# A decoder trunk on one core: output weights gated and summed in the stream's background track, and the output gate's row built by VectorE plus two rounded column sums

## The chip, the core and the metric

The kernel runs on one NeuronCore of one Trainium2 chip. A core has a matrix engine (TensorE, "PE" in the profile; its weight loads stand apart as "PEld"), a vector engine (VectorE, "DVE"), a scalar engine (ScalarE, "ACT"), GpSimd ("POOL") and a sync engine ("SP") that here only issues DMA transfers. POOL issues DMA transfers as well. Each engine works through its own list of instructions in order; semaphores tie the lists together. The metric is the device time of one launch in microseconds, as the median of several runs.

## The reference

One layer on a sequence of 1024 positions with 1024 channels, all in float32, cut to what matters here:

```python
mod = c_act @ ada_w[l] + ada_b[l]                    # c_act = silu(c)
shift, scale, gate = jnp.split(mod, 3, axis=-1)
h = rms_norm(x, norm_w[l]) * (1.0 + scale[:, None, :]) + shift[:, None, :]
proj = h @ w_in[l]                                   # 1024 x 9232
hq, hf, hi, hz, gq, gk, gv, gz, ga, mg = jnp.split(proj, IN_OFFSETS, axis=-1)
y_h = hgrn2_branch(hq, hf, hi, hz, ...)              # 8 heads, gated linear recurrence
y_g = gla_branch(gq, gk, gv, gz, ga, ...)            # 4 heads, gated linear attention
u_h = y_h @ w_branch[l, 0]
u_g = y_g @ w_branch[l, 1]
mg = jax.nn.sigmoid(mg.reshape(B, T, N_BRANCH, D_MODEL))
merged = mg[:, :, 0] * u_h + mg[:, :, 1] * u_g
x = x + gate[:, None, :] * (merged @ w_out[l])
return rms_norm(x, final_norm_w)
```

The change touches the vector `gate`, one row of 1024 numbers, and `w_out`, a 1024 x 1024 matrix. Since `gate` scales the columns of `merged @ w_out`, the kernel multiplies it into the columns of `w_out`.

## The kernel before

Activations lie transposed, 128 channels by 1024 positions. A float32 matrix product is made of three products in a rounded type (`fp32r`): `split()` (L190) rounds a tile on ScalarE (L196, the `hi` part) and takes the rest on VectorE (L197, the `lo` part), and then hi*hi, hi*lo and lo*hi are summed in PSUM.

The program has three parts. First comes a start written in a fixed order, in which `h` and the first products are made. Then comes the **stream** (`Stream.go`): a list of jobs, each a block of the product `h @ w_in`. A `Feat` job (L541) makes 128 channels in 48 matrix instructions; a `Vblk2` job (L643 to L645) makes values of four heads in 192. `go` walks through the jobs and, at each unit of work, calls `weave`, which advances two tracks of generators: `stream.side`, in which the attention of the heads is computed, and `stream.back`, the background track. An entry of a track gives back how many units it wants to wait. Only the first entry of a track is advanced; the next begins when it has ended. Tiles come from `S`, 46 slots of 4 KB per partition, handed out in the order in which they were given back; `ahead` loads the weights of coming jobs while enough slots are free.

Before the change the background track holds `prepare()` (sums for a later stage, whose stores to DRAM are the rows `ws`), and behind it `gate_side()`, which makes the gate's row: eight loads of `ada_w`, eight multiply-adds on VectorE (L1052, L1054) into `gacc`, and then, for each half of 512 columns, two plain float32 matrix instructions (L1062: the column sums of `gacc` with a matrix of ones; L1063: the bias row with a row of ones) and a copy to SBUF (L1064).

The last part, `last_stages` and `out_stage`, makes the remaining products by Strassen-like sums of quarters, 28 groups of (b, p). Its matrix instructions stand at L1343 (`b` 0 to 3) and L1520 (the output product). What happens beside them is hung on points of this walk with `after(b, p, i, f)`. There stands, before the change, the work on `w_out`: for each half kk, `load_wy` loads four tiles of 128 x 1024 through SP (L1466), `gate_wy` multiplies each by the gate's row on VectorE (L1474), `sum_wy` makes four sums in place (L1484), and `keep_wy` stores seven of these tiles to DRAM through POOL (L1469, rows `wo`). Half 0 is hung on group (0, 3) and what follows, half 1 on (1, 1) to (1, 7). The output stage reads the seven products of each half back, from group (3, 7) on.

Around them in this part: the sigmoid gates of branch 1 are made on ScalarE from PSUM (L1414) into half slots, and stored by POOL (L1415, rows `gate`); a half slot can be used again when its store has landed. `build` makes the two parts of an activation factor (L1260 to L1264), `prep_duo` those of a weight (L1285, L1286).

An attention (`attention`) of a head needs, on VectorE, the products L676 to L679 before its first block of small matrix instructions (L683), and L710, L711 before the second (L715). `put_act` stores a head's result through POOL (L916, rows `yh`), and POOL adds its squares (L1107).

Past the start, the order of each engine's list is not the order of the code: a scheduler places the instructions by its own estimates. Calls wrapped in `tc.keep_in_program_order` are held to the code's order.

## Time and profile before

| | before |
|---|---|
| median of 3 runs | 1215.93 us (1215.64 to 1216.92) |
| the profiled execution's own time | 1216.46 us |
| its span, first to last instruction | 1214.8 us |
| TensorE granted clock, mean | 0.998 |
| PE busy | 1184.1 us, 97% |
| VectorE, ScalarE, POOL busy | 790.9, 546.9, 123.8 us |
| HBM read and written | 132.87 and 49.28 MB |

The span is the time inside of which the profile has instructions; 1.66 us of the profiled execution lie around it. Times in the rows are microseconds from the start of the span. A matrix instruction's busy time overlaps its neighbours': what it costs on PE is the distance from its start to the start of the next one. "Idle before" is the time for which the instruction's engine had nothing to do, and the arrow names what ended it.

### The profile page before, as it was taken

To read this page: it belongs to the slowest core of one execution; us is meant where nothing else is said; L and a number is where in the kernel's file an instruction comes from. 1 tells how busy PE (TensorE), PEld (TensorE's weight loads), DVE (VectorE), ACT (ScalarE), POOL (GpSimd) and SP (SyncE) were. 2 spreads that over 40 slices of the span, in tenths; PEclk is the share of its full clock that TensorE was granted. 3 is DMA by queue.
4 is the path that set the end of the run, shared out by engine and by line. 5 is a ranking of instruction groups with operands and counts; after the bars stand their busy time and mean duration, and the time that the engine had idled before them with its cause. 6 is when DMAs were issued, how large, how long until landed. Compare 5 with 4: busy or idle time off the path is not lost.

```text
span 1214.8 us, 20860 instructions
## 1 busy us (share of the span) xinstructions
PE 1184.1 (97%) x8579; PEld 982.6 (81%) x8579; DVE 790.9 (65%) x1245; ACT 546.9 (45%) x797; POOL 123.8 (10%) x215
## 2 busy tenths in 40 slices
PE   5999999999999999999999999999999999999997
PEld 3777889889798888888887888877778888878886
DVE  4637444774848456877884365794653775988994
ACT  5646732434434244344332324455743544444554
POOL 4100000202111121121110101011220000000000
PEclk9999999999999999999999999999999999999999
DMA  9814000844444267255341112054697746435523
GB/s 320 277 70 139 18 19 19 293 141 161 156 152 149 66 207 249 94 179 169 108 174 47 59 53 70 36 174 158 227 343 277 260 160 208 135 104 173 174 104 122
DMA packets 130961, 183.51 MB, mean 151 GB/s; under 512 B 7467, under 2 KB 97633, under 8 KB 130866
## 3 DMA queue, kind: packets, MB, share of 16 engines
q1 hardware_dynamic: 117250, 136.87, 35.7%
q0 software_dynamic: 13568, 45.31, 9.6%
q8 instruction: 67, 1.10, 0.4%
q14 instruction: 28, 0.23, 0.1%
q10 hardware_dynamic: 48, 0.01, 0.0%
HBM read 132.87 MB, written 49.28 MB: 150 GB/s over the span
## 4 chain that ended last, share of the span: by engine, by line
PE 61%; issue 23%; DVE 3%; ACT 3%; POOL 2%; DMA 1%; POOLq 0%; ACTq 0%; DVEq 0%
PE pd L541 19%; PE pd L1343 9%; PE sc_ps L1343 5%; PE pm L1343 5%; PE pd L1520 3%; PE pd L643 2%; PE pd L644 2%; PE pd L645 2%; PE sc_ps L1520 2%; PE pm L848 1%; PE pd L352 1%; PE pm L829 1%; PE pm L850 1%; PE pm L1520 1%; PE sc_ps L352 1%
## 5 line engine op out<-in xcount | busy, mean ns | idle before, releaser
L541 PE MATMUL pd<-b,b 128*128 128x512 f32 x1632 | 387.4, 394 | 0.0
L541 PEld LDWEIGHTS pd<-b,b 128*128 128x128 f32 x1632 | 302.4, 188 | 64.8 <-issue 1.4
L1343 PE MATMUL pd<-b,b 128*128 128x512 f32 x720 | 173.7, 392 | 4.3 <-ACT b L1414 2.1
L1343 PEld LDWEIGHTS pd<-b,b 128*128 128x128 f32 x720 | 133.7, 188 | 35.7 <-ACT b L1414 3.2
L197 DVE TENSOR_TENSOR b<-b,b 128x1024 fp32r<-128x1024 f32 (+2 forms) x89 | 98.9, 1122 | 83.1 <-ACT b L196 65.4
L196 ACT CAST b<-b 128x1024 fp32r<-128x1024 f32 (+2 forms) x89 | 82.9, 948 | 92.1 <-DVE b L1199 14.6
L1286 DVE TENSOR_TENSOR b<-b,b 128x1024 fp32r<-128x1024 f32 x56 | 68.3, 1224 | 66.9 <-ACT b L1285 52.3
L1285 ACT CAST b<-b 128x1024 fp32r<-128x1024 f32 x56 | 58.3, 1050 | 73.9 <-PE pd L1343 20.6
L1343 PE MATMUL sc_ps<-b,b 128*128 128x512 f32 x324 | 79.4, 391 | 1.0 <-ACT scT L793 1.0
L600 PE MATMUL pd<-b,b 128*128 128x256 f32 x256 | 74.2, 290 | 0.0
L1264 DVE TENSOR_TENSOR b<-b,b 128x1024 fp32r<-128x1024 f32 x48 | 59.2, 1251 | 20.8 <-ACT b L1263 15.1
L602 PE MATMUL pd<-b,b 128*128 128x256 f32 x256 | 72.5, 283 | 0.0
L601 PE MATMUL pd<-b,b 128*128 128x256 f32 x256 | 72.4, 283 | 0.0
L1343 PEld LDWEIGHTS sc_ps<-b,b 128*128 128x128 f32 x324 | 60.3, 188 | 14.6 <-ACT scT L793 1.4
L1343 PE MATMUL pm<-b,b 128*128 128x512 f32 x300 | 72.1, 389 | 0.0
L1263 ACT CAST b<-b 128x1024 fp32r<-128x1024 f32 x48 | 49.9, 1050 | 41.2 <-PE pd L1343 16.0
L1343 PEld LDWEIGHTS pm<-b,b 128*128 128x128 f32 x300 | 56.3, 188 | 11.7
L352 PE MATMUL pd<-b,b 128*128 128x512 f32 x192 | 53.3, 410 | 2.0 <-ACT b L196 0.9
L1201 POOL DMA_DIRECT2D ws<-b x64 | 34.6, 541 | 192.0 <-DVE b L1195 86.5
L735 ACT COPY xb<-b 128x512 f32<-128x512 f32 x48 | 29.4, 620 | 49.4 <-PE sc_ps L715 26.7
L643 PE MATMUL pd<-b,b 128*128 128x512 f32 x128 | 51.3, 401 | 0.0
L644 PE MATMUL pd<-b,b 128*128 128x512 f32 x128 | 50.0, 390 | 0.0
(285 smaller groups left out, 1964.3 us busy)
## 6 DMA issues: line engine op xcount, KB each, us to landing
b<-in_w_in_dram SPq DMA_DIRECT2D x66, 512.0 KB, 4.2
ws<-b POOLq DMA_DIRECT2D x64, 256.0 KB, 3.3
b<-ws SPq DMA_DIRECT2D x32, 512.0 KB, 4.9
b<-in_x_dram SPq DMA_DIRECT2D x16, 512.0 KB, 5.7
b<-in_ada_w_dram SPq DMA_DIRECT2D x32, 256.0 KB, 6.9
b<-in_w_branch_dram SPq DMA_DIRECT2D x16, 512.0 KB, 4.4
b<-h SPq DMA_DIRECT2D x14, 512.0 KB, 4.3
wo<-b POOLq DMA_DIRECT2D x14, 512.0 KB, 5.7
```

The lines of the kernel that those rows point to most:

```text
L196: nc.scalar.copy(hi, src)
L197: nc.vector.tensor_sub(lo, src, hi.bitcast(F32))
L352: nc.tensor.matmul(accs[f], wg(a, d, f), b[d][:, half * 512:half * 512 + 512], start=(d == 0 and n == 0), stop=(d == KT - 1 and n == 2))
L541: nc.tensor.matmul(ps[0:w, th * 512:(th + 1) * 512], a[:, k, 0:w], b[:, th * 512:(th + 1) * 512], start=(k == 0 and n == 0), stop=(k == KT ...
L600: nc.tensor.matmul(o, lh, hi[:, k % 4, :], start=(k == 0), stop=False)
L601: nc.tensor.matmul(o, lh, lo[:, k % 4, :], start=False, stop=False)
L602: nc.tensor.matmul(o, ll, hi[:, k % 4, :], start=False, stop=(k == KT - 1))
L643: nc.tensor.matmul(o, lh, hi[:, k % 2, :], start=(k == 0), stop=False)
L644: nc.tensor.matmul(o, lh, lo[:, k % 2, :], start=False, stop=False)
L1286: nc.vector.tensor_sub(lo, t, hi.bitcast(F32))
L1343: nc.tensor.matmul(o, a[:, sl], c, start=(p in (1, 5) and kt == 0 and n == 0), stop=(kt == 3 and n == 2), skip_group_check=True)
L1520: nc.tensor.matmul(o, a, b, start=(p in (1, 5) and kt == 0 and n == 0), stop=(kt == 3 and n == 2), skip_group_check=True)
```

## The change

The lines below are of the changed kernel; line numbers shift by 3 from L1057 on, and by up to 48 behind `out_weights`. In the changed code the bias add is L1057, the two matrix instructions are L1065 and L1066, their copy L1067, `load_wy` issues at L1225, `keep_wy` at L1228, `gate_wy` multiplies at L1233, `sum_wy` adds at L1242; L1079, L1096, L1107 and L1201 of before are L1082, L1099, L1110 and L1206.

```diff
@@ gate_side()
-        yield 3
+        nc.vector.tensor_add(gacc[0:1, :], gacc[0:1, :], gbias[0:1, :])
+        hi, lo = split(gacc)
+        S.free(gacc, gbias)
+        yield 4
         gate_b[0] = S.get([D])
         for half in range(2):
             sl = slice(half * 512, half * 512 + 512)
             pg = mtile()
-            nc.tensor.matmul(pg, ones, gacc[:, sl], start=True, stop=False)
-            nc.tensor.matmul(pg, ones[0:1, :], gbias[0:1, sl], start=False, stop=True)
+            nc.tensor.matmul(pg, ones_r, hi[:, sl], start=True, stop=False)
+            nc.tensor.matmul(pg, ones_r, lo[:, sl], start=False, stop=True)
             nc.scalar.copy(gate_b[0][:, sl], pg)
-        S.free(gacc, gbias)
+        S.free(hi, lo)
@@ hgrn_v(h), done(v)
             if h == 0:
                 stream.back.append([gate_side(), 4])
+                stream.back.append([out_weights(), 4])
@@ gate_wy(kk, n), sum_wy(kk, n): the same instructions, without keep_in_program_order
-        tc.keep_in_program_order(nc.vector.tensor_mul(
-            t, t, gate_b[0][:, f * 512:f * 512 + 512].unsqueeze(1).to_broadcast([P, 2, 512])))
+        nc.vector.tensor_mul(t, t, gate_b[0][:, f * 512:f * 512 + 512].unsqueeze(1).to_broadcast([P, 2, 512]))
-        tc.keep_in_program_order(nc.vector.tensor_add(wy[dst], wy[dst], wy[other]))
+        nc.vector.tensor_add(wy[dst], wy[dst], wy[other])
@@ new
+    def out_weights():
+        for kk in range(2):
+            while len(S.free_list) < 12:
+                yield 1
+            load_wy(kk)
+            yield 8
+            for n in range(4):
+                gate_wy(kk, n)
+                yield 2
+            yield 4
+            for n in range(4):
+                sum_wy(kk, n)
+                yield 3
+            S.free(*wy.values())
+            wy.clear()
@@ behind out_run and out_after
-    for kk, (lead, first, then) in enumerate((((0, 3, 0), (0, 6), (0, 7)), ((1, 1, 2), (1, 5), (1, 6)))):
-        after(*lead, lambda kk=kk: load_wy(kk))
-        after(*((1, 1, 0) if kk == 0 else (1, 7, 3)), drop_wy)
-        for n in range(4):
-            after(*first, n, lambda kk=kk, n=n: gate_wy(kk, n))
-            after(*then, n, lambda kk=kk, n=n: sum_wy(kk, n))
```

How the lists of the engines change is shown at three places. In the names, `b_` is a tile of a slot, `pd` and `pm` are PSUM tiles, and the numbers only tell tiles apart.

On PE, in the stream, where the gate's row is summed between two blocks of the values' product (`pd_5955` is the block that ends, the next `pd` the one that begins). Before:

```order
L645 MATMUL pd_5955<-b_5711,b_158 128x512
L1062 MATMUL pm_6017<-b_5918,ones 128x512
L1063 MATMUL pm_6017<-b_5919,ones 128x512
L1062 MATMUL pm_6021<-b_5918,ones 128x512
L1063 MATMUL pm_6021<-b_5919,ones 128x512
L643 MATMUL pd_6026<-b_5699,b_143 128x512
```

In the change:

```order
L645 MATMUL pd_5955<-b_5711,b_158 128x512
L643 MATMUL pd_6022<-b_5699,b_143 128x512
L644 MATMUL pd_6022<-b_5700,b_143 128x512
L645 MATMUL pd_6022<-b_5699,b_151 128x512
L643 MATMUL pd_6022<-b_5699,b_144 128x512
L644 MATMUL pd_6022<-b_5700,b_144 128x512
L645 MATMUL pd_6022<-b_5699,b_152 128x512
L1065 MATMUL pm_6030<-b_5999,ones_r 128x512
L1066 MATMUL pm_6030<-b_6000,ones_r 128x512
L1065 MATMUL pm_6034<-b_5999,ones_r 128x512
L1066 MATMUL pm_6034<-b_6000,ones_r 128x512
L643 MATMUL pd_6022<-b_5703,b_145 128x512
```

The four instructions take `hi` (`b_5999`) and `lo` (`b_6000`) in place of `gacc` and the bias, and stand six instructions later.

On VectorE, at the same place of the program: `b_5918` is `gacc`, the L1054 rows are its last multiply-adds, and L690 on belongs to head 4's attention behind its first small products. Before:

```order
L1054 SCALAR_TENSOR_TENSOR b_5918<-b_5942,cs,b_5918 128x1024
L197 TENSOR_TENSOR b_6331<-b_5855,b_6330 128x1024
L1054 SCALAR_TENSOR_TENSOR b_5918<-b_5951,cs,b_5918 128x1024
L1054 SCALAR_TENSOR_TENSOR b_5918<-b_5962,cs,b_5918 128x1024
L1054 SCALAR_TENSOR_TENSOR b_5918<-b_5971,cs,b_5918 128x1024
L1054 SCALAR_TENSOR_TENSOR b_5918<-b_5980,cs,b_5918 128x1024
L1054 SCALAR_TENSOR_TENSOR b_5918<-b_5989,cs,b_5918 128x1024
L197 TENSOR_TENSOR b_6440<-b_6233,b_6439 128x1024
L710 TENSOR_TENSOR xb<-b_5669,tot_725 128x128x4
L690 TENSOR_TENSOR blk<-sc_ps,eye_679 128x256
```

In the change:

```order
L1054 SCALAR_TENSOR_TENSOR b_5918<-b_5989,cs,b_5918 128x1024
L1057 TENSOR_TENSOR b_5918<-b_5918,b_5919 1x1024
L197 TENSOR_TENSOR b_6000<-b_5918,b_5999 128x1024
L197 TENSOR_TENSOR b_6344<-b_5855,b_6343 128x1024
L1233 TENSOR_TENSOR b_6247<-b_6247,b_6029 128x1024
L1233 TENSOR_TENSOR b_6249<-b_6249,b_6029 128x1024
L1233 TENSOR_TENSOR b_6251<-b_6251,b_6029 128x1024
L1233 TENSOR_TENSOR b_6253<-b_6253,b_6029 128x1024
L1242 TENSOR_TENSOR b_6247<-b_6247,b_6249 128x1024
L1242 TENSOR_TENSOR b_6249<-b_6249,b_6253 128x1024
L1242 TENSOR_TENSOR b_6253<-b_6253,b_6247 128x1024
L690 TENSOR_TENSOR blk<-sc_ps,eye_679 128x256
```

The bias add, the split of `gacc`, four gatings (`b_6029` is the gate's row) and three of the four sums of half 0 now stand ahead of head 4's attention, which was preceded by the split of a job's weights.

On VectorE, two jobs later, between the end of head 4's attention and the factors of head 5 (L1079 of before, L1082 of the change). Before:

```order
L1096 SCALAR_TENSOR_TENSOR b_6387<-pm_6410,vec,b_6387 128x512
L197 TENSOR_TENSOR b_6868<-b_6645,b_6867 128x1024
L953 TENSOR_TENSOR b_6470<-b_6470,pd_6392 128x1024
L1079 TENSOR_SCALAR b_6528<-b_6528,oml,lb 128x1024
L1080 TENSOR_SCALAR b_6528<-b_6528 128x1024
```

In the change:

```order
L1099 SCALAR_TENSOR_TENSOR b_6400<-pm_6423,vec,b_6400 128x512
L1233 TENSOR_TENSOR b_6682<-b_6682,b_6029 128x1024
L1233 TENSOR_TENSOR b_6684<-b_6684,b_6029 128x1024
L1233 TENSOR_TENSOR b_6688<-b_6688,b_6029 128x1024
L1242 TENSOR_TENSOR b_6682<-b_6682,b_6684 128x1024
L1233 TENSOR_TENSOR b_6686<-b_6686,b_6029 128x1024
L197 TENSOR_TENSOR b_6764<-b_6559,b_6763 128x1024
L953 TENSOR_TENSOR b_6490<-b_6490,pd_6405 128x1024
L1242 TENSOR_TENSOR b_6684<-b_6684,b_6688 128x1024
L1242 TENSOR_TENSOR b_6688<-b_6688,b_6682 128x1024
L1242 TENSOR_TENSOR b_6686<-b_6686,b_6688 128x1024
L1082 TENSOR_SCALAR b_6552<-b_6552,oml,lb 128x1024
```

All eight VectorE instructions on half 1 of `w_out` stand between them, on both sides of L953, the product that empties a `pd` tile. The sums are in place: each also waits until POOL's earlier store of the tile that it overwrites has landed. On POOL, the fourteen stores `wo` stand between the stores `yh` of heads 3, 4 and 5 instead of among the stores `gate`; on SP, the eight loads of `w_out` stand among those of the stream's weights.

More of the change, by code (lines that the diff above doesn't have):

```diff
@@ L1179, in hybrid_trunk_kernel @@
     sources += [[branch(n, d) for d in range(0, 8, 2)] for n in (1, 0)]
+    X_OF = {1: (0, 0), 2: (1, 0), 4: (1, 1)}
     w_sums = [[[dp.tile([P, T], F32, name=f"ws{b}{j}{i}") for i in range(4)] for j in range(2)] for b in range(4)]
@@ L1210, in prepare, with load_wy, keep_wy, gate_wy @@
                 yield from weight_sums(b, i)
+    w4_d = {p: [dp.tile([P, T], F32, name=f"wo{p}{kk}") for kk in range(2)] for p in OUT_PRODUCTS}
+    w_rows = w_out[0].rearrange("(i two p) c -> two p i c", two=2, p=P)
+    wy = {}
+    def load_wy(kk):
+        for kh in range(2):
+            for f in range(2):
+                t = wy[kh, f] = S.get([2, 512])
+                nc.sync.dma_start(t, w_rows[kh][:, 2 * kk:2 * kk + 2, f * 512:f * 512 + 512])
+    def keep_wy(p, kk, kh, f):
+        nc.gpsimd.dma_start(w4_d[p][kk], wy[kh, f].rearrange("p a f -> p (a f)"))
+    def gate_wy(kk, n):
+        kh, f = ((0, 0), (0, 1), (1, 0), (1, 1))[n]
+        t = wy[kh, f]
+        nc.vector.tensor_mul(t, t, gate_b[0][:, f * 512:f * 512 + 512].unsqueeze(1).to_broadcast([P, 2, 512]))
+        for p, at_ in X_OF.items():
+            if at_ == (kh, f):
+                keep_wy(p, kk, kh, f)
+        if kk == 1 and n == 3:
+            S.free(gate_b[0])
+    def sum_wy(kk, n):
+        p, dst, other = ((7, (0, 0), (0, 1)), (5, (0, 1), (1, 1)), (6, (1, 1), (0, 0)), (3, (1, 0), (1, 1)))[n]
+        nc.vector.tensor_add(wy[dst], wy[dst], wy[other])
+        keep_wy(p, kk, *dst)
+    def out_weights():
[13 more added lines that the diff above has]
+            wy.clear()
     stream.back.append([prepare(), 60])
@@ L1218, in hybrid_trunk_kernel @@
     BUILT = [g for g in GROUPS if g[0] != 1]
-    X_OF = {1: (0, 0), 2: (1, 0), 4: (1, 1)}
     BANK = {1: "a", 2: "a", 5: "e", 3: "e", 6: "b", 7: "b", 4: "b"}
@@ L1456, in hybrid_trunk_kernel @@
         after(*((2, 5) if d % 2 else (1, 4)), d // 2, lambda d=d: load_gate1(d))
-    w4_d = {p: [dp.tile([P, T], F32, name=f"wo{p}{kk}") for kk in range(2)] for p in OUT_PRODUCTS}
-    w_rows = w_out[0].rearrange("(i two p) c -> two p i c", two=2, p=P)
-    wy, w4_raw, W4 = {}, {}, {}
-    def load_wy(kk):
-        for kh in range(2):
-            for f in range(2):
-                t = wy[kh, f] = S.get([2, 512])
-                nc.sync.dma_start(t, w_rows[kh][:, 2 * kk:2 * kk + 2, f * 512:f * 512 + 512])
-    def keep_wy(p, kk, kh, f):
-        nc.gpsimd.dma_start(w4_d[p][kk], wy[kh, f].rearrange("p a f -> p (a f)"))
-    def gate_wy(kk, n):
-        kh, f = ((0, 0), (0, 1), (1, 0), (1, 1))[n]
-        t = wy[kh, f]
-        tc.keep_in_program_order(nc.vector.tensor_mul(
-            t, t, gate_b[0][:, f * 512:f * 512 + 512].unsqueeze(1).to_broadcast([P, 2, 512])))
-        for p, at_ in X_OF.items():
-            if at_ == (kh, f):
-                keep_wy(p, kk, kh, f)
-        if kk == 1 and n == 3:
-            S.free(gate_b[0])
-    def sum_wy(kk, n):
-        p, dst, other = ((7, (0, 0), (0, 1)), (5, (0, 1), (1, 1)), (6, (1, 1), (0, 0)), (3, (1, 0), (1, 1)))[n]
-        tc.keep_in_program_order(nc.vector.tensor_add(wy[dst], wy[dst], wy[other]))
-        keep_wy(p, kk, *dst)
-    def drop_wy():
-        S.free(*wy.values())
-        wy.clear()
+    w4_raw, W4 = {}, {}
     def load_w4(p):
```

## The prediction

> **What bounds the kernel now.** I read the page first: the share of each engine, then the chain of work that ended last.

> ```profile
> PE 1184.1 (97%) x8579; PEld 982.6 (81%) x8579; DVE 790.9 (65%) x1245; ACT 546.9 (45%) x797; POOL 123.8 (10%) x215
> PE 61%; issue 23%; DVE 3%; ACT 3%; POOL 2%; DMA 1%; POOLq 0%; ACTq 0%; DVEq 0%
> ```

> PE is busy for 97% of the span, and the chain runs over PE. So an edit pays in one of two ways: it shortens what stands in PE's list, or it ends a stretch in which PE stands still. Work taken off VectorE, POOL or a DMA queue pays only through the second. The next view is the busy time by stretch: first the place in the stream to which the change brings its work, then the stage from which it takes it. The columns are the stretch, the busy time and instructions of PE, PEld, DVE, ACT and POOL, the granted clock, the DMA share and GB/s.

> ```profile
> 640.00:710.00 70.00, 70.00 (x546) 56.01 (x545) 23.75 (x47) 21.15 (x34) 3.44 (x3) 1.00 0.18 50
> 800.00:960.00 160.00, 155.17 (x923) 126.25 (x922) 95.54 (x116) 84.79 (x120) 20.98 (x35) 1.00 0.70 240
> ```

> In the stream PE never stops, VectorE is busy a third of the time and the DMA engines 18%. Between 800 and 960 PE lacks 4.8 us (160 less 155.17) and the DMA engines are at 70%. What PE waits for there is the view of its waits in that stretch (total, times, longest):

> ```profile
> PE pd L1343 <- ACT b L1414: 2.1, 2, 1.8
> PE pd L1343 <- DVE b L953: 1.5, 1, 1.5
> PE sc_ps L1343 <- ACT scT L793: 1.0, 1, 1.0
> PE pd L1343 <- ACT b L1315: 0.2, 1, 0.2
> ```

> So there is 4.8 us to be won from waits, in four rows, and the granted clock is 1.00 on both sides: no term comes from the clock.

> **Term 1, the gate's row on PE.** The timeline of PE shows the four plain float32 matrix instructions between their neighbours (start, duration; two to a row where the records touch), and the second fence a sum of exactly the form that the change puts there: two instructions by two with the rounded ones, 128x512 each.

> ```profile
> 640.69 0.39 PE L645 MATMUL pd<-b,b 128*128 128x512 f32 x1
> 640.92 1.02 PE L1062 MATMUL pm<-b,ones 128*128 128x512 f32 x2
> 643.98 1.12 PE L1063 MATMUL pm<-b,ones 1*128 1x512 f32 x2
> 645.02 0.50 PE L643 MATMUL pd<-b,b 128*128 128x512 f32 x1
> 645.36 0.39 PE L644 MATMUL pd<-b,b 128*128 128x512 f32 x1
> ...
> 854.39 0.40 PE L964 MATMUL pm<-b,ones_r 128*128 128x512 f32 x1
> 855.39 2.92 PE L1343 MATMUL sc_ps<-b,b 128*128 128x512 f32 x12
> ```

> An ordinary instruction costs 0.23 us (640.69 to 640.92). The four take 640.92 to 645.02 = 4.10 us, and the instruction behind them is followed after 0.34 instead of 0.23, so 0.11 more: 4.21 us. The rounded four take 854.39 to 855.39 = 1.00 us. PE's list is short of 4.21 - 1.00 = **3.2 us**, in a stretch without any idle time, so all of it counts unless something new makes PE wait.

> [...]

> What can be late here is `lo`: the four instructions now need the bias add, the ScalarE cast and the VectorE rest behind the last multiply-add.

> ```profile
> 631.27 1.23 DVE L197 TENSOR_TENSOR b<-b,b 128x1024 fp32r<-128x1024 f32 x1
> 632.41 6.56 DVE L1054 SCALAR_TENSOR_TENSOR b<-b,cs,b 128x1024 f32<-128x1024 f32 x5
> 643.02 0.58 ACT L1064 COPY b<-pm 128x512 f32<-128x512 f32 x1 [0.90 <-PE pm L1063]
> 644.08 1.04 ACT L196 CAST b<-b 128x1024 fp32r<-128x1024 f32 x1 [0.47 <-PE pm L1062]
> ```

> The order of VectorE puts that L197 behind the L1054 rows, so these end at about 631.3 + 6.5 = 637.8; an add over 1024 columns and one partition costs no more than the 1.2 of a full tile (639.0), the cast 1.04 (640.0), the rest 1.23 (641.3). PE comes to the four after six more instructions, 640.92 + 6 x 0.23 = 642.3. One microsecond is left; if it is not enough, the four would stand later and cost up to about 1.2.

> **Term 2, the work on `w_out` in the stream.** Sixteen VectorE instructions, eight loads and fourteen stores move. Their rows before, with the time from a DMA's issue to its landing:

> ```profile
> L1474 DVE TENSOR_TENSOR b<-b,b x8: 1218/1218/1225, 861.8 to 922.0; 128x1024 f32<-128x1024 f32 x8
> L1469 POOL DMA_DIRECT2D wo<-b x14: 531/537/547, 863.3 to 959.1; - x14
> DMA to landing us min/median/max: 4.0/5.7/7.6
> ```

> VectorE has 46 us free of 70 at the new place; 16 x 1.22 = 19.5 us fit in total. What matters is the order: an in-place sum waits until POOL's store of its tile has landed, and VectorE holds everything behind it. The two neighbours on PE that need VectorE, around half 0 (head 4) and around half 1 (head 5), with the VectorE rows ahead of them:

> ```profile
> 654.78 1.31 PE L683 MATMUL sc_ps<-xb,b 128*32 128x80 f32 x64
> 661.68 0.89 PE L715 MATMUL sc_ps<-xb,b 128*32 128x48 f32 x64
> 656.38 0.42 DVE L690 TENSOR_TENSOR blk<-sc_ps,eye 128x256 f32<-128x256 f32 x1
> 658.10 0.47 DVE L711 TENSOR_TENSOR xb<-xb,tot 128x256 f32<-128x256 f32 x1
> 697.31 1.23 DVE L197 TENSOR_TENSOR b<-b,b 128x1024 fp32r<-128x1024 f32 x1 [6.54 <-DMA yh<-b]
> 710.90 0.82 DVE L1079 TENSOR_SCALAR b<-b,oml,lb 128x1024 f32<-128x1024 f32 x1 [9.66 <-ACT b L1077]
> 716.70 0.64 DVE L679 TENSOR_TENSOR xb<-xb,b 128x256 f32<-128x256 f32 x1
> 717.89 1.31 PE L683 MATMUL sc_ps<-xb,b 128*32 128x80 f32 x64
> ```

> *Half 0.* The row is on PE by 643.3, and a ScalarE copy behind it makes it 643.7. Four gatings at 1.2 end at 648.5; POOL's store of the last of them, which the third sum overwrites, lands 4.0 to 7.6 later, 652.5 to 656.1, and the sum ends 1.2 behind that, 653.7 to 657.3. L690 could start at 654.78 + 1.31 - 3.2 = 652.9, and L715's inputs must stand at 661.68 - 3.2 = 658.5. From L690 on VectorE needs some 3 us to the end of L711 (0.7 for the L710 that now stands behind it, and 2.2 from 656.38 to 658.57), so it may start as late as 655.5. PE stalls for 0 to 1.8. The DMA engines are at 18% here and at 70% where 5.7 was the median; I take the landing near its minimum, and **0**.

> *Half 1.* Its loads wait for slots that come free at about 691 to 694, from the stores `yh` among others. With 4 to 7 us to land, the gatings run from 698 to 703, the stores of the last land by 707 to 711, and the last sum would end at 705 to 709.4 (its own tile's store is an earlier one). L1082 could start at 710.90 - 3.2 = 707.7, and behind it VectorE has to come to L679's end by the time PE reaches L683, where 717.89 less 717.34 leaves 0.5. So the stall is 0 to 1.2 if the loads and stores come as in the stream, up to 2.5 at the late ends of all rows; again I take **0**, nearest to the 18% share.

> Both gatings and sums read two SBUF tiles, and POOL squares a tile near by. Such a meeting is in the trace: the same form of VectorE instruction, L686, elsewhere 0.95, took 2.51 us beside a POOL product.

> ```profile
> 624.37 3.62 POOL L1107 TENSOR_TENSOR b<-b,b 128x1024 f32<-128x1024 f32 x1
> 626.29 2.51 DVE L686 TENSOR_TENSOR b<-xb,b 128x768 f32<-128x768 f32 x1
> 717.77 0.95 DVE L686 TENSOR_TENSOR b<-xb,b 128x768 f32<-128x768 f32 x1
> ```

> That is 1.56 more for one instruction at half 1; it stands ahead of loads that come later anyway, and I add nothing. [...]

> **Term 3, what leaves the last stages.** 8 loads and 14 stores of 512 KB, 11.5 MB of the 38 MB (240 GB/s over 160 us) that move there, and 19.5 us of VectorE. Where the longest wait comes from is shown by the chain in that window:

> ```profile
> 883.76 0.53 POOL wo L1469
> 887.31 4.81 DMA gate<-b
> 892.22 0.61 ACT b L1414
> 892.87 3.02 PE pd L1343 x12
> ```

> POOL issues a `wo` store, then the store of a gate's half slot, which needs 4.81 us; ScalarE waits for that half slot, and PE for ScalarE. Without the `wo` stores the gate's store issues no later and has the DMA engines to itself. The wait is 1.8 us long; I take **-1.5**, between nothing (the store's 4.81 stays, since its issue follows another event) and 1.8. The waits on L953 and L793 stay: the first is VectorE's work for an attention, ahead of all `w_out` gating, the second follows another store of `gate`:

> ```profile
> 828.34 1.06 ACT L1260 ACTIVATE b<-b 128x1024 fp32r<-128x1024 f32 x1 [3.59 <-DMA gate<-b]
> ```

> No `wo` store runs then (the first issues at 863.3). Only the order around them is made anew; bounds -0.6 to +1.5 (one more cast ahead of the masks), and I take **+0.3**.

> **Sum.** 1214.8 - 3.2 + 0 - 1.5 + 0.3 = 1210.4 us of span. With the 1.66 around it this execution would read 1212.1; it was 0.53 above the median of the runs, so the forecast is **1211.5 us**.

> **The rivals.**

> *B, only PE's own gain.* The stage re-forms its waits: the half slot's store is issued late for another reason, and the 1.8 stays or moves on. For it: the wait hangs on one slot out of 46, and three more groups of waits stand close to it. Against it: the DMA share falls by nearly a third. 1215.9 - 3.2 = 1212.7, up to 1214.5 with one new wait of half 0 or half 1 (1.8).

> *C, the other side: VectorE waits for POOL's stores ahead of attention.* The in-place sums stand in VectorE's list ahead of head 4's L690 and head 5's L1082. If stores land at the maximum of 7.6 and the loads late, PE loses 1.8 at L715 and 2.5 at L683, and where the stage gives nothing back the time is 1215.9 - 3.2 + 1.8 + 2.5 = 1217.0; each microsecond by which two stores behind each other land later than these rows is added to it. It decides against the change from the point where the two losses pass 3.2; for half 1 alone, where the last sum ends later than 707.7 + 0.5 + 3.2 = 711.4. For it: in-place stores are the one wait of DMA length put ahead of PE's inputs. Against it: at 18% DMA the minimum of 4.0 is the nearer row.

> *D, all four waits of the stage go.* They hang together in time: with POOL's and VectorE's lists shorter, all 4.8 us could vanish: 1215.9 - 3.2 - 4.8 = 1207.9. For it: the DMA share. Against it: three of four stand ahead of the first `wo` store.

> *The change doesn't do what it says:* the four stand where `lo` isn't ready, and half of the gain is a wait. Then it is 1211.5 + 1.2 = 1212.7, inside B.

> **How the numbers follow.** The forecast A has 0.50 (1209.5 to 1213), B 0.25, C 0.12, D 0.13. A measurement of this kernel tells 0.2% (2.4 us) from no change, so faster ends at 1213.5 and slower begins at 1218.4. A, D and half of B lie below: 0.75. The rest of B and half of C lie between: 0.19 with rounding. Slower keeps the half of C in which stores land later than any row here: 0.06. The range leaves out most of C and the far part of D: 1208 to 1215.5; A's own is 1209.5 to 1213.

> **What would show it.** Right: L1065 and L1066 take 1.0 us on PE with no wait ahead of them, PE's busy time falls by 3.2; the windows 640 to 720 show PE without idle time; the wait on L1414 near 890 is gone. Wrong: a wait of PE on L679 or L711 with VectorE standing at L1242 behind DMA `wo`; PE waiting at L1066 for L197; the stage keeping its 4.8 us; or a wait elsewhere in the stream, from slots that `w_out` holds while jobs want to load weights.

## The result, and the profile after

The changed kernel takes 1222.64 us (median of 6 runs, 1220.34 to 1226.09) against 1215.93 us before (1215.64 to 1217.28). The ratio is 1.0057, with a 95% interval of 1.0041 to 1.0074: slower by 6.7 us, where 4.4 us less were forecast. The profiled execution of the change is the longest of its six, so its rows can show more of each loss than the median does.

The page of the change, its busy times (its span is 1224.2 us, against 1214.8 before):

```profile
PE 1186.9 (97%) x8575; PEld 987.0 (81%) x8575; DVE 793.4 (65%) x1247; ACT 548.5 (45%) x798; POOL 124.4 (10%) x215
```

PE's busy time has grown by 2.8 us although its list has become 3.2 us shorter. Instructions of the same kind must have become slower somewhere. The timeline of PE at the gate's row shows that it isn't there (start, duration):

```profile
641.79 0.39 PE L1065 MATMUL pm<-b,ones_r 128*128 128x512 f32 x1
642.02 0.39 PE L1066 MATMUL pm<-b,ones_r 128*128 128x512 f32 x1
642.25 0.40 PE L1065 MATMUL pm<-b,ones_r 128*128 128x512 f32 x1
642.49 0.39 PE L1066 MATMUL pm<-b,ones_r 128*128 128x512 f32 x1
642.72 0.39 PE L643 MATMUL pd<-b,b 128*128 128x512 f32 x1
```

The four instructions take 0.93 us (641.79 to 642.72), with no wait ahead of them. The busy time by stretch shows where the rest went: first three stretches of the kernel before, then the same of the change (columns as in the prediction: PE, PEld, DVE, ACT, POOL, granted clock, DMA share, GB/s).

```profile
710.00:725.00 15.00, 15.00 (x142) 12.01 (x144) 13.89 (x25) 5.61 (x7) 0.00 (x0) 1.00 0.25 70
800.00:830.00 30.00, 28.38 (x345) 22.41 (x344) 25.53 (x44) 16.56 (x23) 1.83 (x3) 1.00 0.42 142
890.00:910.00 20.00, 18.18 (x80) 14.74 (x79) 6.31 (x7) 8.87 (x14) 3.77 (x7) 1.00 1.00 358
```

```profile
640.00:710.00 70.00, 70.00 (x557) 58.29 (x556) 46.11 (x69) 22.75 (x35) 10.91 (x17) 1.00 0.59 197
710.00:725.00 15.00, 11.85 (x104) 9.49 (x103) 11.33 (x20) 3.00 (x4) 0.00 (x0) 0.89 0.24 82
800.00:830.00 30.00, 27.05 (x277) 21.25 (x275) 26.87 (x46) 14.57 (x20) 3.05 (x2) 0.89 0.51 174
890.00:910.00 20.00, 17.32 (x69) 13.83 (x68) 5.65 (x6) 7.07 (x10) 2.96 (x6) 0.91 0.68 211
```

From 640 to 710, where the work on `w_out` now lies, PE is still never idle, with VectorE at 46 us and the DMA engines at 59%. Behind it PE loses 3.2 us in 710 to 725. And in three stretches the granted clock is 0.89 to 0.91 where it was 1.00. PE's waits from 640 to 960 in the change:

```profile
PE sc_ps L683 <- DVE xb L679: 3.2, 1, 3.2
PE pd L1391 <- ACT b L1462: 3.0, 2, 2.7
PE pd L1391 <- DVE b L953: 3.0, 1, 3.0
PE pd L1391 <- ACT b L1363: 1.2, 1, 1.2
PE sc_ps L1391 <- ACT scT L793: 1.0, 1, 1.0
PE pd L1391 <- DVE b L1378: 0.9, 1, 0.9
```

Two rows are new (L683, L1378), three have grown (L1363 is L1315 of before: 0.2 became 1.2; L1462 is L1414 of before: its longest wait went from 1.8 to 2.7; L953: 1.5 became 3.0). Pairing the same PE instruction of both traces gives the account in start times, change minus before: -3.8 us behind the gate's row (-0.5 is there ahead of it already, -3.3 comes from the row); +3.3 at L683 (717.89 before, 717.35 after) and +1.5 by 721; +1.8 at the wait on L953 and +2.7 within the 6 us behind it; +1.4 by 858, at L1363; +0.3 and +1.2 at L1378 and L1462, and +1.5 within 5 us of the latter. With the stretches between it comes to +9.8. The parts behind a wait and without one of their own (by 721, within 6 us, within 5 us), 1.5 + 2.7 + 1.5 = 5.7, are stretches where every instruction takes longer. Two windows behind the first wait show it, with the DMA engines idle and PE without a gap:

```profile
718.00:720.00 2.00, 2.00 (x41) 1.64 (x31) 1.86 (x4) 0.93 (x2) 0.00 (x0) 0.52 0.00 0
720.00:722.00 2.00, 2.00 (x7) 1.56 (x6) 2.00 (x5) 0.00 (x0) 0.00 (x0) 0.63 0.00 0
```

The chain of waits around 705 to 719 tells what L683 waited for:

```profile
702.54 3.27 DMA wo<-b
...
705.87 0.34 SPq L1278
...
706.30 7.96 DMA b<-in_w_in_dram
...
714.35 1.05 ACT b L196
...
715.43 1.23 DVE b L197
716.65 0.56 DVE xb L679
717.22 0.14 issue
717.35 1.76 PE sc_ps L683 x64
```

Not for `w_out`: for a weight of a later job, whose split (L196, L197) stands ahead of L679 in VectorE's list. Its load was issued by SP at 706.30, behind a load of `h` (L1278) that had waited for a store of `w_out` to land, and it needed 7.96 us. Before the change the load of the same weight was issued well ahead of this place, and its L197 started without any wait, 1.1 us ahead of L679:

```profile
715.57 1.21 DVE L197 TENSOR_TENSOR b<-b,b 128x1024 fp32r<-128x1024 f32 x1
```

### The profile page after: what moved, and what is told of

Its sections match the earlier page's. It is cut to its first block, busy times and chain, and to the rows that moved or that the text cites. A ratio compares the mean times of both kernels' runs of the same rounds, so it can differ in the third digit from the quotient of the medians.

```text
span 1224.2 us, 20849 instructions
## 1 busy us (share of the span) xinstructions
PE 1186.9 (97%) x8575; PEld 987.0 (81%) x8575; DVE 793.4 (65%) x1247; ACT 548.5 (45%) x798; POOL 124.4 (10%) x215
## 4 chain that ended last, share of the span: by engine, by line
PE 59%; issue 22%; DMA 4%; ACT 3%; DVE 3%; POOL 2%; SPq 0%; POOLq 0%; ACTq 0%; DVEq 0%
PE pd L541 16%; PE pd L1391 10%; PE sc_ps L1391 5%; PE pm L1391 5%; PE pd L1537 3%; PE pd L643 2%; PE pd L644 2%; PE pd L645 2%; DMA b<-in_w_in_dram 2%; PE sc_ps L1537 2%; PE pm L848 1%; PE pm L829 1%; PE pm L850 1%; PE pd L352 1%; PE pm L1537 1%
## 5 line engine op out<-in xcount | busy, mean ns | idle before, releaser
L197 DVE TENSOR_TENSOR b<-b,b 128x1024 fp32r<-128x1024 f32 (+2 forms) x90 | 99.2, 1114 | 79.0 <-ACT b L196 66.2
L196 ACT CAST b<-b 128x1024 fp32r<-128x1024 f32 (+2 forms) x90 | 84.0, 949 | 111.0 <-PE pd L541 19.9
L1206 POOL DMA_DIRECT2D ws<-b x64 | 34.6, 541 | 192.0 <-DVE b L1200 86.5
L643 PE MATMUL pd<-b,b 128*128 128x512 f32 x128 | 51.2, 400 | 0.0
L644 PE MATMUL pd<-b,b 128*128 128x512 f32 x128 | 50.0, 390 | 0.0
```

The costliest lines, as they stand in the source:

```text
L196: nc.scalar.copy(hi, src)
L197: nc.vector.tensor_sub(lo, src, hi.bitcast(F32))
L643: nc.tensor.matmul(o, lh, hi[:, k % 2, :], start=(k == 0), stop=False)
L644: nc.tensor.matmul(o, lh, lo[:, k % 2, :], start=False, stop=False)
```

## The experiments

The runs are called E1 to E11 below. The theory after this reading, called "slots": the tiles of `w_out` take slots in the stream, so that other tiles get slots which come free late, and the load or cast that stands there holds its queue.

**One part alone.** The gate's row without the move (`e1_row_only`: the kernel before with the first hunk of the diff), and the move with the row as before (`e2_wout_only`: the change without that hunk).

> The kernel before with the gate's row as in the change; the work on w_out stays in the last stages. Theory 'slots' (the loss comes from w_out's tiles in the stream: loads and casts that stand in order behind a slot which a store gives back late, and a lower clock after each long wait of PE): PE's list is shorter by 3.2 us and nothing else moves, 1212.7 us, ratio 0.9974, and PE has no wait on L679 near 714. Rival 'row' (the split on VectorE and ScalarE upsets the order of the engines): 1216 us or more.

Measured: 1213.19 us, ratio 0.9963 (0.9949 to 0.9977). No wait on L679. The 3.2 us that were forecast for the row lie inside the measured interval, a gain of 2.8 to 6.2.

> The changed kernel with the gate's row as before (four plain float32 matrix instructions). Theory 'slots': the same queue of SP, so the same waits as in the change and 3.2 us more on PE, 1222.6 + 3.2 = 1225.8 us (1223.5 to 1229, since the change's own runs spread over 5.7 us); PE waits some 3 us for L679 with a lower clock behind it. Rival 'row': without the new row the loss is gone, 1216 us or less.

Measured: 1222.07 us, ratio 1.0040 (1.0026 to 1.0054). The loss is in the move, so "row" falls. But 1225.8, with 1223.5 as its lower bound, was a miss: with the row the change isn't faster than without it (1.0057 and 1.0040, overlapping). PE waits 2.3 us for L679 here and 3.2 in the change, where it arrives earlier at something that a transfer sets; for the gate's half slot it waits 1.3 here and 2.7 there. The clock takes a part too. The wait of 1.3 us is followed by none lower (1.00 from 890 to 910), that of 2.7 in the change is (0.91 there). In the profiled execution, the longest of its ten, the waits of 2.3 and 2.2 us (L679, L953) are followed by a lower clock as well (0.89 from 710 to 725, 0.94 from 800 to 830); but the five shortest of its ten runs have a mean clock of 0.998 or 0.999, and of the change's six runs only the shortest has 0.998, the others 0.992 to 0.996. So this kernel loses its time mostly by the waits themselves, and the change by the clock as well.

**The place in SP's queue.** `e3_h_on_pool`:

```diff
-            nc.sync.dma_start(raw_f[g][kk], f_x[p][kk])
+            (nc.gpsimd if g in GROUPS[:2] else nc.sync).dma_start(raw_f[g][kk], f_x[p][kk])
```

> The changed kernel; only the four loads of h for the first two groups of the last stages, two of which wait on SP for stores of w_out ahead of a weight of the stream, are issued by POOL. Slots and everything else stay. Theory 'slots': the weight's load issues at about 699 instead of 706.3, PE's wait of 3.2 us for L679 and the 1.5 us of low clock behind it are gone, and the waits in the last stages stay: 1222.6 - 4.7 = 1217.9 us (1215.5 to 1220). Rival 'in-place sums' (VectorE stands for its own stores ahead of attention): the wait stays, 1222.6 us. Rival 'transfers' (the DMA engines are too full at 700 to 715 for the weight to be in time): the wait is shorter but over 1.5 us.

Measured: 1219.81 us, ratio 1.0013 (1.0000 to 1.0027). The time lies in the range, but the reason was wrong in part. PE still waits 1.6 us for L679, and the chain shows why:

```profile
699.93 5.68 PE pd L541 x25
705.62 0.02 issue
705.63 7.07 DMA b<-in_w_in_dram
```

With nothing ahead of it on SP the load is issued at 705.63, not at 699: its own slot is let go by PE only then. So the queue cost 0.7 us, and the slot that the weight was given is late. But the landing has its part: it took 7.07 us, where the load of the same weight took 4.8 in E9 and E10 (issued at 685.6 and 689.9). The rival "transfers" had asked for a shorter wait of over 1.5 us, and that is what came. An estimate from these rows: the way from landing to L683 is 3.1 us (712.70 to 715.80), PE stands there at 714.2, and 705.63 + 4.8 + 3.1 = 713.5, so with a landing of 4.8 PE wouldn't have waited. The late slot made the wait possible, and the slow landing made it come. The clock stayed at 1.00 behind this shorter wait; behind the waits on L953 (2.2) and for the half slot (2.3) it still fell, to 0.94 from 800 to 830 and 0.91 from 890 to 910.

**Giving the slots back late.** `e4_free_late`:

```diff
                 sum_wy(kk, n)
                 yield 3
+            yield 24
             S.free(*wy.values())
```

> The changed kernel; the slots of w_out's tiles are given back 24 units of work after the last sum instead of at once, when their stores have long landed, and half 1 begins that much later. Theory 'slots': no load stands behind a store of w_out any more, so no wait on L679 over 1.5 us after half 1 and no low clock there: 1217.9 us or less (1212 to 1219; how the slots fall out in the last stages is open). Rival 'in-place sums' or 'transfers': half 1 makes the same wait where it now stands, 1221 us or more.

Measured: 1215.14 us, ratio 0.9979 (0.9967 to 0.9991). The weight now has another slot and there is no wait on L679 at all; the clock is 1.00 in every stretch behind 640. The weight's load is issued at 689.0. In the last stages two of the waits stay (L1364, which is L1363 of the change, 1.0 us; L1379, which is L1378, 1.2).

**The change again, on the chip of the next three.**

> The changed kernel, unedited, beside the runs below on one chip. Theory 'slots': 1.004 to 1.007 of the kernel before, PE's wait for L679 near 714 over 2.5 us with a granted clock under 0.95 right behind it. The clock theory (a wait of PE of some 2.3 us or more is followed by microseconds at a lower granted clock, one of 2.0 or less is not) says which of its waits are followed by a low clock; without it, waits and clock have nothing to do with each other.

Measured: 1222.89 us, ratio 1.0051 (1.0033 to 1.0069). Its waits for L679 (2.5 us), L953 (2.1) and L1462 (2.6) are each followed by a stretch of lower clock (0.89, 0.94 and 0.91 in the windows used above), those of 1.2 us or less by none.

**Half 0 alone in the stream.** `e6_half0`: `out_weights` runs over `range(1)`, and half 1 hangs on the last stages as before the change.

> The changed kernel with half 0 alone in the stream; half 1 is loaded, gated and summed in the last stages, as before. Theory 'slots': the queue of SP has no load behind a store of half 1, so no wait on L679 near 714; half 0's own stores land long before its slots are used again. 1212.7 us (1211 to 1216), ratio 0.994 to 1.000. Rival: any w_out work in the stream upsets the order of the last stages; then the new waits on the copies (ACT near 851, VectorE near 880, 2.3 us in the change) stay and the ratio is over 1.000.

Measured: 1211.67 us, ratio 0.9959 (0.9948 to 0.9970). PE's waits from 640 to 960 that are left:

```profile
PE pd L1395 <- DVE b L953: 1.5, 1, 1.5
PE sc_ps L1395 <- ACT scT L793: 0.9, 1, 0.9
PE pd L1395 <- ACT b L1466: 0.3, 1, 0.3
```

The wait for the gate's half slot, 1.8 us before the change, is gone, and no new one has come. This is the fastest kernel of the study, together with the row alone, from which its interval doesn't part it: what half 0's move gains beyond the row is seen in the waits, not in the time.

**Room or order in the last stages.** `e7_hold_slots`: `e4_free_late`, and

```diff
+    after(0, 3, 0, lambda: hold(0))
+    after(1, 1, 0, lambda: let_go(0))
+    after(1, 1, 2, lambda: hold(1))
+    after(1, 7, 3, lambda: let_go(1))
```

where `hold` takes four slots off the list and `let_go` puts them back.

> The change with the slots given back late (as in the run before), and in the last stages four free slots are set aside from group (0, 3) to (1, 1) and from (1, 1) to (1, 7), as w_out's tiles held them before the change; no instruction is added. Theory 'slots' for the stage: with the old room the loads and casts stand as before, the new waits near 851 and 880 (2.3 us) go, and the time falls from 0.998 to 0.996 of the kernel before. Rival 'order' (the lists are made anew by the missing VectorE and POOL instructions, not by the room): the same waits, 0.998 or more.

Measured: 1216.36 us, ratio 0.9997 (0.9984 to 1.0009). Room isn't it: against E4 the wait on L1379 grew from 1.2 to 2.9 us (with a clock of 0.89 from 875 to 890), and that on L1364 is still there, 0.7 after 1.0.

**A longer wait, to test the clock.** `e8_longer_wait`, an edit of the kernel before:

```diff
         nc.scalar.activation(g, ap, AF.Sigmoid)
+        if d == 3 and summed:
+            nc.gpsimd.tensor_mul(g, g, ones[:, 0:1].to_broadcast([P, 512]))
         nc.gpsimd.dma_start(gate1_d[d][:, half * 512:half * 512 + 512], g)
```

> The kernel before; one POOL product with ones (128x512, some 1.2 to 1.8 us) stands ahead of the two stores of gate 3 in half slots, so that PE's wait near 890 (1.98 us longer than the usual distance, granted clock 1.00 behind it) becomes 3.2 to 3.8 us. Clock theory: the granted clock falls below 0.95 within 15 us behind it and the time grows by the 1.2 to 1.8 and another 1.5 to 2.7, 2.7 to 4.5 us in all. Rival (the low clocks of the changed kernel come from something else): the clock stays at 1.00, and at most 1.8 us is lost.

Measured: 1220.34 us, ratio 1.0026 (1.0013 to 1.0039): 3.2 us (1.6 to 4.7). PE's row at this wait before and with the edit, and the window behind it with the edit:

```profile
892.87 3.02 PE L1343 MATMUL pd<-b,b 128*128 128x512 f32 x12 [1.82 <-ACT b L1414]
```

```profile
894.42 4.22 PE L1343 MATMUL pd<-b,b 128*128 128x512 f32 x12 [3.15 <-ACT b L1414]
```

```profile
890.00:910.00 20.00, 16.84 (x67) 13.43 (x66) 5.96 (x6) 7.04 (x11) 4.11 (x8) 0.91 0.95 326
```

The wait grew by 1.33 us, and the same twelve instructions behind it now take 4.22 us instead of 3.02, at a clock of 0.91 over the window where it was 1.00. So this wait, made longer, is followed by a lower clock (0.91), with the rest of the lists in the same order; the time alone wouldn't tell, since its interval reaches below the 1.8 us of the rival. But the upper bound that went with the theory (2.3 us or more is followed by a low clock) fails in this same trace, and the lower one (2.0 or less is not) fails in E11, with 1.97 and a clock of 0.66 behind it. The wait on L953 is longer here than before, too, and the clock behind it stays at 1.00:

```profile
812.29 3.92 PE L1343 MATMUL pd<-b,b 128*128 128x512 f32 x16 [2.37 <-DVE b L953]
```

```profile
812.00:832.00 20.00, 19.58 (x248) 15.59 (x249) 15.42 (x35) 8.09 (x12) 1.09 (x2) 1.00 0.20 72
```

**Who gets the late slot.** `e9_weight_first`:

```diff
+            if kk:
+                stream.jobs[stream.loaded].load()
+                stream.loaded += 1
             load_wy(kk)
```

> The changed kernel; only, ahead of half 1's four loads the next weight of the stream is loaded, so that it takes the slot that half 1's first tile had, and half 1's last tile takes the slot that the weight had, which PE lets go at 705.6. Theory 'slot' (who gets that slot is late; the place in SP's queue and the crowd of transfers matter less): the weight lands by 695 and nothing waits for it; the last tile lands at about 710.6, its gating and the three sums behind it, which wait for stores, end at about 718 ahead of head 5's factors, L679 ends at about 724, and PE waits some 10 us there with a low clock behind it: 1222.6 + 7 = 1230 us or more. Rival 'crowd' (the weight was late because so many transfers ran beside it): the weight is in time, half 1 gains from nothing but loses little, 1220 us or less.

Measured: 1226.26 us, ratio 1.0086 (1.0071 to 1.0101). The weight is loaded at 685.6 and nothing waits for it, and PE's wait for L679 grew to 5.7 us instead of the 10 expected: half 1's last tile got a slot that was free at 694.7, not at 705.6, so it was not the slot that the weight had in the change; other tiles had been handed out between. The chain there:

```profile
704.92 6.91 DMA wo<-b
...
711.91 1.24 DVE b L1242
```

Here it is the in-place sums that wait for a store ahead of head 5's factors. "Crowd" as it was put (1220 or less) falls: with the weight in time the kernel became slower. But "slot" missed its 1230 as well, and slow transfers are in this wait, too: the store needed 6.91 us, where half 0's seven stores in the change landed in 2.9 to 4.7.

**Half 1 alone in the stream.** `e10_half1`: `out_weights` waits 44 units and runs over half 1; half 0 hangs on the last stages.

> The changed kernel with half 1 alone in the stream, at the place in the code where it stands in the change; half 0 is done in the last stages, as before. The weight of the stream that was late takes a slot that POOL lets go before 690. Theory 'slot': no wait on L679 near 714 although half 1's loads, gatings, sums and stores are all there; 1216 us or less. Rival 'half 1' (its transfers and in-place sums in front of head 5 are what is late, whatever the slots): the wait stays at 1.5 us or more, 1217 us or more. Whether the new waits near 851 and 880 come with half 1 is open; by 'order' they may.

Measured: 1214.18 us, ratio 0.9988 (0.9978 to 0.9998). No wait near 714, though all loads, gatings, sums and stores of half 1 stand in the stream. They also stand earlier here: the last load is issued at 681.0 and the last store at 696.2, in the change at 693.7 and 706.1. So half 1 can be had there at little cost, but slot and time moved together in this run. A wait of 1.3 us for L679 of head 6 (near 758), the 1.5 us on L953 and smaller ones in the last stages are left.

**Half 1 twice.** `e11_half1_twice`: the change, with half 1 loaded, gated, summed and stored again at its old place; the added work only writes the same values again.

> The changed kernel, with half 1 done a second time in the last stages as before the change (loaded, gated, summed, stored over the same values); the gate's row keeps its slot until then. It tells where the new waits of the last stages near 851, 880 and 898 (1.3, 1.0 and 0.8 us more than before) come from. Theory 'absence' (the lists come out in another order because half 1's VectorE and POOL instructions are missing there): they go, and the time falls by about 3 us in spite of the added work, ratio 1.000 to 1.003. Theory 'carried over' (they come from the stream, whose loads and attention reach the last stages later): they stay, ratio 1.004 or more. In both the wait near 714 stays at 1.5 us or more, since a weight still follows half 1's tiles.

Measured: 1216.57 us, ratio 1.0003 (0.9990 to 1.0016), though PE waits for L679 twice (3.2 us near 714, 1.97 near 762). Its waits from 640 to 960:

```profile
PE sc_ps L683 <- DVE xb L679: 5.1, 2, 3.2
PE pd L1395 <- DVE b L953: 2.4, 1, 2.4
PE sc_ps L1395 <- ACT scT L793: 0.5, 1, 0.5
PE pd L1395 <- ACT b L1466: 0.3, 1, 0.3
```

All three waits in question are gone, so "absence" holds; the time fell by some 6 us against the change, more than the 3 expected. Room was put back here as well, but E7 shows that room alone doesn't do it; the transfers that came back with the instructions weren't tried apart. How it works is seen on ScalarE near 850. The copies that free PSUM are L1315 before, L1363 in the change, L1367 here. First the kernel before, then the change, then half 1 twice:

```profile
850.46 0.58 ACT L1315 COPY b<-pd 128x512 f32<-128x512 f32 x1
852.22 1.05 ACT L196 CAST b<-b 128x1024 fp32r<-128x1024 f32 x1 [1.18 <-POOL b L1107]
```

```profile
855.39 1.06 ACT L196 CAST b<-b 128x1024 fp32r<-128x1024 f32 x1 [1.15 <-POOL b L1110]
856.35 1.04 ACT L1311 CAST b<-b 128x1024 fp32r<-128x1024 f32 x1
857.29 0.58 ACT L1363 COPY b<-pd 128x512 f32<-128x512 f32 x1
```

```profile
856.67 0.59 ACT L1367 COPY b<-pd 128x512 f32<-128x512 f32 x1
858.38 1.05 ACT L196 CAST b<-b 128x1024 fp32r<-128x1024 f32 x1 [1.12 <-POOL b L1110]
```

L196 waits for POOL's sum of squares. Before, the copy that PE needs stands ahead of it; in the change it stands behind it and behind a cast. With the second half 1 in place it is ahead again.

## Why the prediction was wrong

**Term 1 was right.** The four instructions took 0.93 us where 1.00 was forecast, six instructions later, and `lo` was in time. E1 gains what the term says. What failed is the thought that this gain counts whole: here it did so only up to the next wait that a transfer sets. E2 and the change differ by those 3.2 us of PE and came out alike (1222.07 and 1222.64 us).

**Term 2, half 0: right at 0.** E6 holds it: PE without a gap from 640 to 725, at a clock of 1.00. The landing "near its minimum" was a fair choice: the seven stores landed in 2.9 to 4.7 us.

**Term 2, half 1: this step failed.** It was worked out on VectorE and POOL alone, and there it came out nearly as said (the loads issued earlier, from 685.6 to 693.7). The last sum and the factors behind it in the change:

```profile
704.53 1.23 DVE L1242 TENSOR_TENSOR b<-b,b 128x1024 f32<-128x1024 f32 x1 [1.02 <-DMA wo<-b]
707.14 0.81 DVE L1082 TENSOR_SCALAR b<-b,oml,lb 128x1024 f32<-128x1024 f32 x1 [1.39 <-ACT b L1080]
```

The sum ends at 705.8 (705 to 709.4 was the range), and L1082 isn't held by it: it waits for ScalarE. What was not worked out is what eight loads take from the list of slots: half 1's four tiles took four of them ahead of the stream's next weights, one weight was left with a slot that PE still read until 705.6, and its split stood ahead of L679. The weight's load then took 7.96 us to land, among the stores and loads beside it. The 0 was +3.3 in the profiled run. "A wait elsewhere in the stream, from slots" stood only in the last sentence, without a price. The runs in which the weight got another slot (E4, E6, E7, E9, E10) issue its load at 685.6 to 689.9, and PE waits for it in none of them; in the change, E2, E3, E5 and E11 it is issued at 705.6 to 710.0, and PE waits behind its split in all five. By the estimate at E3 the late slot alone wouldn't have been enough: the slow landing or the queue of SP came on top.

**Term 3: the -1.5 was right for a kernel that was not the change.** It is what the profile of E6 shows: with half 0's transfers gone and half 1 still there, the 1.8 us for the half slot fell to 0.3 at most. In the change the same wait became 2.7, that on L1363 went from 0.2 to 1.2, 0.9 us came new at L1378, and the wait on L953, which was to stay, doubled to 3.0. The "+0.3 for the order" (bounds -0.6 to +1.5) was the mis-sized term. E7 and E11 show that it isn't room alone: with half 1's work gone from the last stages, the lists of ScalarE and VectorE there come out in another order; why the scheduler then places the copies later was not followed up.

**"No term comes from the clock": wrong.** The granted clock was 1.00 in the profile before, where no wait from 640 to 960 is longer than 1.82 us. In the change three are, of 2.7 to 3.2, and 5.7 of the profiled run's 9.4 us are the slow instructions behind them; the mean clock of the change's six runs goes from 0.992 to 0.998 (0.993 in the profiled one, 0.998 in the shortest, 1220.34 us), so this part differs from run to run. By the account above, 8.0 us of longer waits and 5.7 us of slow instructions stand against the 3.8 that PE was ahead.

**The rivals.** C had the right sign and the wrong mechanism: its in-place waits cost PE nothing in the change (VectorE stood 3.9 us for stores in all). They are real one step further on: in E9 they made the 5.7 us. B had the stage right (its waits re-formed), but not the clock. D and "doesn't do what it says" did not happen.

**Left open.** The wait on L953 at the start of the last stages is 1.5 to 3.0 us in kernels whose lists are the same there (1.5 before, 2.4 in E8), so it lies on both sides of the lengths behind which the clock fell. The record of the runs speaks for this as a part of the spread: of the 31 runs of the kernel before beside E1, the two longest (1221.0 and 1221.5 us) have a mean clock of 0.995 and 0.994, all others 0.997 to 0.999. Why the wait differs between such runs was not tried. Why the weight took 7 to 8 us to land in the change, E2, E3 and E5, and not the 4.8 of E9 and E10, was not separated either; that the transfers beside it did it is an estimate, since no run took them away alone.

## What to carry to other kernels

When work that takes buffers from a shared list is moved, follow the buffers and not only the engines: ask which load will get the buffer that is free last, and what stands behind that load in the order of the engine that needs it. Work taken out of a stage can change the scheduler's order there even if it cost nothing, so the stage it leaves has to be read again, too. And a wait of the matrix engine should be priced with what follows it: here waits of 2.7 to 3.2 us cost another 1.2 to 2.7 us behind them, one of 1.8 us only itself; a gain that only made PE arrive earlier at such a wait was no gain (1222.64 us in the change, 1222.07 in E2).

## What the runs showed of the hardware

Behind some waits of PE the granted clock fell for some microseconds (in the change to 0.50, for 3.41 or 6.83 us), and the length of the wait alone doesn't say behind which. In the thirteen profiles of this case, from 640 to 960 us, no wait of up to 1.82 us (before) is followed by a lower clock, and every wait of 2.5 us or more is (2.51 in E5 to 5.66 in E9). Of the ten between, 1.97 and 2.37 (E11), 2.09 (E5), 2.17 and 2.31 (E2), 2.24 and 2.31 (E3) and 2.34 us (E1) are followed by it, 2.27 (E9) and 2.37 (E8, shown above) are not. The lowest that is, in E11, with the window behind it:

```profile
764.58 1.31 PE L683 MATMUL sc_ps<-xb,b 128*32 128x80 f32 x64 [1.97 <-DVE xb L679]
```

```profile
765.00:770.00 5.00, 5.00 (x63) 4.05 (x55) 4.86 (x11) 2.01 (x4) 0.00 (x0) 0.66 0.01 3
```

What parts them may be seen in the traces' own record of the clock. The change from 714 us on, cut where its clock changes (and 3.41 us ahead of each fall):

```profile
714.65:718.07 3.42, 0.72 (x41) 0.75 (x45) 2.64 (x4) 0.75 (x1) 0.00 (x0) 1.00 0.26 102
718.07:721.48 3.41, 3.41 (x41) 2.70 (x31) 3.27 (x6) 0.93 (x2) 0.00 (x0) 0.50 0.00 0
721.48:810.23 88.75, 88.69 (x885) 73.92 (x884) 60.88 (x116) 37.19 (x59) 7.95 (x6) 1.00 0.26 79
810.23:813.64 3.41, 1.41 (x6) 0.80 (x5) 3.41 (x4) 3.41 (x5) 0.00 (x0) 1.00 0.30 124
813.64:820.47 6.83, 5.88 (x14) 4.64 (x15) 6.83 (x13) 2.25 (x4) 0.00 (x0) 0.50 0.24 77
820.47:898.97 78.50, 74.59 (x511) 60.12 (x509) 40.19 (x58) 47.18 (x69) 9.38 (x14) 1.00 0.49 158
898.97:902.39 3.42, 1.15 (x5) 0.96 (x6) 1.23 (x1) 2.22 (x4) 1.07 (x2) 1.00 0.10 40
902.39:905.80 3.41, 3.41 (x10) 2.64 (x9) 1.23 (x1) 0.00 (x0) 0.00 (x0) 0.50 0.66 198
```
